# Between the two layers: one block of tokens ahead of the other, values before keys, and the residual's weight and bias on VectorE

## The chip, the cores and the metric

The kernel runs on one core of one Trainium2 chip. A core has a matrix engine (TensorE, "PE" in the profile, with its weight loads as "PEld"), a vector engine (VectorE, "DVE"), an activation engine (ScalarE, "ACT"), GpSimd ("POOL") and SyncE ("SP"), from whose queue every DMA of this kernel is issued. Each engine runs its own instructions in order and waits on semaphores for the others. The metric is the time of one execution on the device in microseconds (us). Three executions of the kernel before took 1293.49, 1297.56 and 1298.24 us; their median is 1297.56.

## The reference: what is computed

256 tokens of width 2048 pass through two layers. The first is a state-space mixer (Mamba-2), the second an attention with three dilated windows. Around each stands the same frame, and between them one matrix of 2048 x 6144 makes the keys and values that the second layer uses:

```python
for layer in range(DEPTH):
    shift, scale, gate = _adaln(c, ada_w[layer], ada_b[layer])
    h = x * (1.0 + scale) + shift
    if layer < N_A_LAYERS:
        y = _ssd_mixer(h, ...)
    else:
        y = _dilated_mixer(h, k_sh, v_sh, b_in_w[i], b_out_w[i])
    x = _layer_norm(DEEPNORM_ALPHA * x + (1.0 + gate) * y, ln_g[layer], ln_b[layer])
    if layer == N_A_LAYERS - 1:
        k_sh, v_sh = _shared_kv(x, kv_w)
```

`_layer_norm` subtracts a token's mean, divides by its standard deviation, multiplies by a weight and adds a bias. `_adaln` is a product of one vector with a matrix of 2048 x 6144 for each layer. Keys and values have three groups of eight heads of 128 each. All numbers are float32.

## The kernel before, in words

**Precision and weights.** A float32 product is made of three products of a shorter format: high part by high part, high by low, low by high. Every weight comes from HBM in pieces of 128 x 1024 words. `split` (lines 90 to 96) makes its high part on ACT (line 93, `whi`) and its low part on DVE (line 95, `wlo`); it has six buffers for raw pieces and four for each part. Activations are kept as high and low parts, too (`xhi`, `xlo`).

**Three forms of product.** `tm_mults` (lines 166 to 176, results with tokens on partitions) takes a block of 128 tokens as PE's stationary operand and streams 512 columns of weights, three matmuls for each block and each 128 of depth; it is used for the state-space layer's z, both output projections and the values. `cm_piece` (lines 109 to 121) and `cm_wide` (lines 140 to 157) have results with channels on partitions: 128 x 128 weights are stationary and tokens are streamed. `cm_piece` streams 256 tokens three times; `cm_wide` streams high and low parts of the tokens together, 512 columns against the weight's high part, then 256 against its low part. Keys must have channels on partitions.

**The step between the layers.** The first layer's output projection (line 683) runs over four chunks of 512 columns with 16 pieces each (two k-tiles of 128 to a piece). In the last chunk the last two pieces are held back (`split_end=2`) and multiplied for block 0 of the tokens first, then for block 1, so block 0's accumulator is complete earlier. `residual` (line 662) multiplies by the gate, adds the scaled input and takes partial moments (lines 664 to 666). `ln_scale` (line 668) makes the factors of both blocks together, with an inverse square root of eleven small DVE steps (lines 209 to 215). Then block 0 is normalised by ACT and block 1 by DVE, in place (lines 701 and 703), and `x_tiles` (line 712) brings the result to channels on partitions: transposes on PE (line 716), weight and bias on ACT into `xhi` (line 719) and on DVE into a copy (line 720), from which the low part is taken (line 721).

**Keys and values.** The keys of the first four heads of each group come first, in the `cm_piece` form, all three groups at once piece by piece (`cm_quads`, line 741), with the next two tiles of x made ahead of each round. Then come the other keys by `cm_wide` and the six value chunks by `tm_chunk` (line 755). Their results go to four large tiles (`kk0`, `kk1`, `vt0`, `vt1`).

**Work in the background.** The modulation (`ada_dot`, line 251) is 48 columns for the second layer, each a DMA of 128 x 2048 words and one DVE instruction. `queue` makes a list of such jobs, and `background` runs some of them after each weight piece: 16 in the output projection, one to three pieces, 32 under the second keys and the values, four to nine pieces. After the values, GpSimd multiplies the residual by the norm's weight and adds its bias (lines 773 and 774), from rows loaded and spread over the partitions.

**Second layer.** `queries` (24 wide pieces for four heads) and `attend` run twice, then `z_gate`, then the output projection. For its end a tile is filled with the gate and the last norm's weight and bias rows (line 850); then two chunks are multiplied, the pieces of the other two are split and held, and block 0 is finished before block 1.

**What sets the order.** A scheduler decides the order on each engine before the run. It takes instructions that are ready by its estimate of time, those that come earlier in the program first, and so may place later work between two dependent steps. `tc.issue_after(ins)` forbids that: what is written in the block on the engine of `ins` is queued behind `ins`. On the chip each engine keeps that order.

## Time and profile before

| | |
|---|---|
| median of three runs | 1297.56 us (1293.49 to 1298.24) |
| the profiled execution's own time | 1296.34 us |
| its span, first to last instruction | 1294.5 us |
| PE busy | 1247.4 us, 96% |
| PE weight loads busy | 1097.5 us, 85% |
| DVE busy | 1027.1 us, 79% |
| ACT busy | 707.7 us, 55% |
| POOL busy | 27.5 us, 2% |
| mean granted PE clock | 0.994 |
| DMA | 335.86 MB, mean 259 GB/s |

The profile is that of one execution. A row of a timeline gives start, duration, engine, line of the kernel and operation, result and operands, shape, and in brackets the idle time before it and what ended that. In the chain a row gives start, the time that it adds, and what. A row of a group ends with busy time, the mean of one in ns and idle time before. A row of windows gives a stretch, its length, then for PE, PEld, DVE, ACT and POOL the busy time with the number of instructions in brackets, and at its end the granted PE clock, the DMA engines' busy share and GB/s. Matmuls are pipelined: their durations overlap, so the distance between two starts is what one of them costs.

The stages by time: the first layer's input and scan up to about 550 us, its output projection to 731, keys and values from 740 to 1015, queries and attention to about 1200, the gate and the second output projection to the end.

### The profile page before, as it was taken

How to read it: one execution, taken by the hardware profiler on the slowest of the kernel's cores; microseconds unless marked ns; L12 is line 12 of the kernel's file. 1: busy time of each engine (PE TensorE's matmuls, PEld its weight loads, DVE VectorE, ACT ScalarE, POOL GpSimd, SP SyncE). 2: the span in 40 equal slices, each digit the busy share in tenths (PEclk: the TensorE clock that was granted, in tenths of full speed). 3: DMA queues.
4: the chain of work that ended last, by engine and by line, in shares of the span. 5: the costliest groups of instructions: out<-in, count | busy, mean ns of one | idle time of the engine just before them, and what ended most of it. 6: DMA issues, size and time to landing. Idle time of an engine off the chain costs nothing.

```text
span 1294.5 us, 19393 instructions
## 1 busy us (share of the span) xinstructions
PE 1247.4 (96%) x7414; PEld 1097.5 (85%) x7414; DVE 1027.1 (79%) x1453; ACT 707.7 (55%) x1033; POOL 27.5 (2%) x20
## 2 busy tenths in 40 slices
PE   4999999999999999999999799999999999999997
PEld 4879988899898999878888699888887888888885
DVE  6789887999999778899765577888777757758778
ACT  3545457867587687864333444444435644444651
POOL 0000000000000000000000043000000000000000
PEclk9999999999999999999999899999999999999999
DMA  9999967696884546398977575999897854363471
GB/s 382 422 398 419 374 210 243 219 342 248 290 313 170 183 161 212 128 338 326 385 258 218 190 238 170 338 393 365 329 342 275 275 187 155 98 187 107 147 276 65
DMA packets 80445, 335.86 MB, mean 259 GB/s; under 512 B 8960, under 2 KB 9056, under 8 KB 67552
## 3 DMA queue, kind: packets, MB, share of 16 engines
q1 hardware_dynamic: 80352, 334.62, 71.5%
q8 instruction: 58, 0.95, 0.3%
q14 instruction: 35, 0.29, 0.1%
HBM read 332.41 MB, written 2.18 MB: 258 GB/s over the span
## 4 chain that ended last, share of the span: by engine, by line
PE 81%; DVE 9%; DMA 5%; ACT 3%; issue 2%; SPq 0%; DVEq 0%; ACTq 0%
PE acc L151 12%; PE acc L174 11%; PE acc L175 11%; PE acc L173 11%; PE acc L121 8%; PE acc L119 8%; PE acc L120 8%; PE acc L152 6%; DMA araw<-in_ada 4%; DVE wlo L95 2%; DVE araw L251 2%; PE py L593 2%; PE aux L802 1%; ACT whi L93 1%; PE po L816 1%
## 5 line engine op out<-in xcount | busy, mean ns | idle before, releaser
L95 DVE TENSOR_TENSOR wlo<-raw,whi 128x1024 fp32r<-128x1024 f32 x395 | 484.4, 1239 | 188.5 <-ACT whi L93 187.5
L93 ACT ACTIVATE whi<-raw 128x1024 fp32r<-128x1024 f32 x395 | 413.0, 1056 | 334.3 <-PE acc L175 139.0
L119 PE MATMUL acc<-actT,whi 128*128 128x256 f32 x960 | 274.1, 289 | 23.2 <-ACT whi L93 19.3
L174 PE MATMUL acc<-wlo,actT 128*128 128x512 f32 x704 | 276.7, 393 | 3.2 <-DVE wlo L95 3.1
L121 PE MATMUL acc<-actT,wlo 128*128 128x256 f32 x960 | 270.8, 286 | 4.4 <-DVE wlo L95 4.4
L173 PE MATMUL acc<-whi,actT 128*128 128x512 f32 x704 | 272.2, 394 | 0.8 <-ACT actT L648 0.7
L120 PE MATMUL acc<-actT,whi 128*128 128x256 f32 x960 | 272.9, 286 | 0.0
L151 PE MATMUL acc<-actT,whi 128*128 128x512 f32 x704 | 251.6, 400 | 0.0
L251 DVE SCALAR_TENSOR_TENSOR araw<-araw,cb__72 128x2048 f32<-128x2048 f32 x96 | 219.3, 2286 | 17.9 <-DMA araw<-in_ada 17.5
L119 PEld LDWEIGHTS acc<-actT,whi 128*128 128x128 f32 x960 | 186.6, 196 | 25.1 <-ACT whi L93 20.3
L152 PE MATMUL acc<-actT,wlo 128*128 128x256 f32 x704 | 201.6, 286 | 0.1
L121 PEld LDWEIGHTS acc<-actT,wlo 128*128 128x128 f32 x960 | 184.6, 194 | 6.7 <-DVE wlo L95 6.4
L120 PEld LDWEIGHTS acc<-actT,whi 128*128 128x128 f32 x960 | 186.7, 194 | 0.4 <-DVE actT L398 0.2
L175 PE MATMUL acc<-whi,actT 128*128 128x512 f32 x448 | 175.0, 391 | 0.0
L174 PEld LDWEIGHTS acc<-wlo,actT 128*128 128x128 f32 x704 | 132.3, 188 | 33.5 <-DVE wlo L95 7.0
L151 PEld LDWEIGHTS acc<-actT,whi 128*128 128x128 f32 x704 | 132.4, 188 | 30.9
L173 PEld LDWEIGHTS acc<-whi,actT 128*128 128x128 f32 x704 | 131.8, 188 | 28.5 <-ACT actT L648 1.5
L152 PEld LDWEIGHTS acc<-actT,wlo 128*128 128x128 f32 x704 | 133.2, 189 | 0.8 <-DVE wlo L95 0.4
L175 PE MATMUL acc<-whi,ylo 128*128 128x512 f32 x256 | 100.3, 392 | 0.0
L175 PEld LDWEIGHTS acc<-whi,actT 128*128 128x128 f32 x448 | 84.1, 188 | 17.1
L175 PEld LDWEIGHTS acc<-whi,ylo 128*128 128x128 f32 x256 | 48.0, 188 | 9.5
L320 DVE SCALAR_TENSOR_TENSOR cacc<-acc,prm,cacc 128x253 f32<-128x253 f32 (+2 forms) x96 | 42.0, 474 | 5.5 <-ACT cacc L317 5.2
(212 smaller groups left out, 1093.0 us busy)
## 6 DMA issues: line engine op xcount, KB each, us to landing
araw<-in_ada SPq DMA_DIRECT2D x96, 1024.0 KB, 7.4
raw<-in_win SPq DMA_DIRECT2D x160, 512.0 KB, 5.3
raw<-in_wkv SPq DMA_DIRECT2D x72, 512.0 KB, 6.2
raw<-in_wout SPq DMA_DIRECT2D x64, 512.0 KB, 4.9
raw<-in_wbin SPq DMA_DIRECT2D x64, 512.0 KB, 4.3
raw<-in_wk SPq DMA_DIRECT2D x24, 512.0 KB, 8.6
cbc<-cumd SPq DMA_DIRECT2D x16, 512.0 KB, 5.4
raw<-in_wbout SPq DMA_DIRECT2D x16, 512.0 KB, 3.7
```

The source lines that it names most:

```text
L93: S.activation(hi, raw, AF.Copy)
L95: latest[0] = V.tensor_tensor(lo, raw, hi.bitcast(F32), op=ALU.subtract)
L119: T.matmul(o, hi[:, k, c_], ahi[:, kt, :], start=first, stop=False, skip_group_check=True)
L120: T.matmul(o, hi[:, k, c_], alo[:, kt, :], start=False, stop=False, skip_group_check=True)
L121: T.matmul(o, lo[:, k, c_], ahi[:, kt, :], start=False, stop=kt == k1 - 1, skip_group_check=True)
L151: T.matmul(ps[n], hi[:, k, c_], xp[:, kt], start=kt == 0, stop=False, skip_group_check=True)
L152: T.matmul(ps[n][:, 0, :], lo[:, k, c_], xhi[:, kt, :], start=False, stop=kt == KT - 1, skip_group_check=True)
L173: T.matmul(o, h_, hi[:, k, :], start=kt == k0, stop=False, skip_group_check=part)
L174: T.matmul(o, h_, lo[:, k, :], start=False, stop=False, skip_group_check=part)
L175: end = T.matmul(o, l_, hi[:, k, :], start=False, stop=kt == k1 - 1, skip_group_check=part)
L251: V.scalar_tensor_tensor(raw, raw, 1.0, cb_, op0=ALU.mult, op1=ALU.mult, accum_out=mod[layer][:, ct, j:j + 1])
L320: V.scalar_tensor_tensor(acc[:, o:], ps[:, :L - o], w[:, j:j + 1], acc[:, o:], op0=ALU.mult, op1=ALU.add)
```

## The change

What it does, in order of the program:

- In the last output chunk four pieces are held for the two blocks instead of two. Each block gets its moments on its own (`moments`, which stood at the kernel's end, with the shorter `rsqrt1`), and its first 512 columns are normalised at once.
- Four pieces of value weights are loaded and split during that chunk (`first_weights`), into the buffers of the first layer's y tiles, which now live in a pool of eight places (`slots`) and later hold keys, values and held weights.
- x is brought to channels on partitions for block 0 alone in its first four tiles; the values of groups 0 and 1 are multiplied for block 0 with the four pieces, then the same for block 1; from the third piece on both blocks go together.
- Values of the first heads come first, then all keys in the wide form, then the other values. `cm_quads` is gone. The wide form does its two 512-column matmuls before its two 256-column ones.
- 11 modulation columns, one to four pieces, lie in the output projection, and 37, one to two pieces, in the keys and values; none in the first two value chunks.
- The residual's norm weight and bias go from GpSimd, after the values, to DVE, one operation after each of 16 pieces of the first queries (`weigh`), with the rows in the buffer that attention uses later (`pT`).
- At the end the gate row is loaded behind the first output chunk, the norm rows behind the second and fourth of the held pieces, and the multiplications by the norm's weight (`scaled`) come behind all the splits.

```diff
@@ cm_wide
                 for n in range(2):
-                    c_ = slice(n * P, n * P + P)
-                    T.matmul(ps[n], hi[:, k, c_], xp[:, kt], start=kt == 0, stop=False, skip_group_check=True)
-                    T.matmul(ps[n][:, 0, :], lo[:, k, c_], xhi[:, kt, :], start=False, stop=kt == KT - 1,
+                    T.matmul(ps[n], hi[:, k, n * P:n * P + P], xp[:, kt], start=kt == 0, stop=False,
+                             skip_group_check=True)
+                for n in range(2):
+                    T.matmul(ps[n][:, 0, :], lo[:, k, n * P:n * P + P], xhi[:, kt, :], start=False, stop=kt == KT - 1,
                              skip_group_check=True)
...
+    slots = ctx.enter_context(tc.tile_pool(name="slots", bufs=1))
...
-        y = [pa.tile([P, 2, 512], F32, name=f"y{g}") for g in range(G)]
+        y = [slots.tile([P, 2, 512], F32, name=f"s{g}") for g in range(G)]
...
+        def moments(b, k, diag=None):
+            mv = sm.tile([P, 2], F32, name=f"e{b}mv", bufs=1)
+            V.bn_aggr(mv, st[b][:, 0:k, :])
...
+            r = rsqrt1(ve, f"e{b}")
...
+        def normalise(b, c0_, c1_):
+            (r, nb), cs_ = norm[b], slice(c0_, c1_)
+            if b == 0:
+                S.activation(u[b][:, cs_], u[b][:, cs_], AF.Identity, bias=nb, scale=r)
+            else:
+                V.tensor_scalar(u[b][:, cs_], u[b][:, cs_], r, nb, op0=ALU.mult, op1=ALU.add)
+
+        def first_weights(q):
+            if q % 3 == 2 and q < 12:
+                i = q // 3
+                into = [slots.tile([P, 1024], F32R, name=f"s{2 * i + j}") for j in range(2)]
+                first_v.append(split(load_piece(wv[2 * (i % 2)][i // 2]), into=into))
...
-                          nk=2 * KT, rate=(1, 3) if n else (0, 1), pre=None if n else y_ahead,
-                          split_end=2 if n == 3 else 0)
+                          nk=2 * KT, rate=(1, 4) if n else (0, 1),
+                          pre={0: y_ahead, 3: first_weights}.get(n), split_end=4 if n == 3 else 0)
             if n == 0:
-                queue(pn, cols1[:16])
+                pin[0] = latest[-3].ins
+                state[0] = 0
+                queue(pn, cols1[:11])
...
                 residual(n, ps[b], b, (gt, u[b][:, 512 * n:512 * n + 512]), xr)
-        drain()
-        r, nb, nb_last = ln_scale()
...
+                if n == 3:
+                    norm.append(moments(b, 4))
+                    normalise(b, 0, 256)
+                    normalise(b, 256, 512)
...
-        cm_quads([(wkv[2 * g], ps[g]) for g in range(NG)], xhi, xlo, pre=ahead, after=nb_last.ins)
...
+        vps = [tm_pair(), tm_pair()]
+        for b in range(2):
+            for kt in range(4):
+                tile4 = x_tile(kt, (b,))
+            for n in range(1, 4):
+                normalise(b, 512 * n, 512 * n + 512)
+            for i, w in enumerate(first_v):
+                if b and i == 2:
+                    x_tile(4)
+                    x_tile(5)
+                tm_mults(i // 2, w, vps[i % 2], hx, lx, 0, KT, (b,))
+        for q in range(2, KT // 2):
+            if q < KT // 2 - 1:
+                x_tile(2 * q + 2)
+                x_tile(2 * q + 3)
+            for j in range(2):
+                w = split(load_piece(wv[2 * j][q]), after=tile4.ins if q == 2 else None)
+                tm_mults(q, w, vps[j], hx, lx, 0, KT, range(2))
+        for g in range(2):
+            evict_v(0, g, vps[g])
+
+        R = (1, 2)
...
+            queue(pl, cols1[11:])
             jobs.append(lambda: gate_out(1))
...
+            evict_v(0, 2, tm_chunk(wv[4], hx, lx, rate=R))
             for hq in range(2):
                 for g in range(NG):
...
+                    for w in range(2):
+                        cm_wide(wk[2 * (2 * g + hq) + w], kv[hq, g][:, 2 * w:2 * w + 2, :], rate=R)
+            for g in range(NG):
+                evict_v(1, g, tm_chunk(wv[1 + 2 * g], hx, lx, rate=R))
...
-                PO.tensor_tensor(u[b][:, cs_], u[b][:, cs_], lnr[0], op=ALU.mult)
-                PO.tensor_tensor(u[b][:, cs_], u[b][:, cs_], lnr[1], op=ALU.add)
...
+    def weigh(n, b, i):
+        if b == 0 and i == 0:
+            t = pc2.tile([P, NG, 384], F32, name="pT", bufs=1).rearrange("p g n -> p (g n)")
+            lnr[n] = [t[:, 512 * j:512 * j + 512] for j in range(2)]
+            for j in range(2):
+                bcast(lnr[n][j], lnrow, j * D + 512 * n)
+        cs_ = slice(512 * n, 512 * n + 512)
+        with tc.issue_after(late):
+            V.tensor_tensor(u[b][:, cs_], u[b][:, cs_], lnr[n][i], op=(ALU.mult, ALU.add)[i])
...
+    jobs.extend(lambda n=n, b=b, i=i: weigh(n, b, i) for n in range(4) for i in range(2) for b in range(2))
...
-                cm_wide(wbin[2 * (2 * g + hq) + w], qq[:, g, 2 * w:2 * w + 2, :])
+                cm_wide(wbin[2 * (2 * g + hq) + w], qq[:, g, 2 * w:2 * w + 2, :], rate=(1, 1))
...
-    bcast(gt[:, 0, :], gated[1])
-    for i in range(2):
-        bcast(lnt[:, i, :], lnrow, (2 + i) * D)
...
         ps = tm_chunk(wbout[n], *og, nk=H)
+        if n == 0:
+            with tc.issue_after(latest[-1].ins):
+                bcast(gt[:, 0, :], gated[1])
         for b in range(2):
             join(n, ps[b], b)
-        scaled(1, chunk[n])
...
+        if i in (1, 3):
+            with tc.issue_after(latest[-1].ins):
+                bcast(lnt[:, i // 2, :], lnrow, (2 + i // 2) * D)
+    for n in range(2):
+        scaled(1, chunk[n])
```

148 lines of the change are left out of this document (52 added, 96 removed).

## The prediction

> **What bounds the kernel now.** I read the page first: its share of busy time, its slices, its chain.
>
> ```profile
> span 1294.5 us, 19393 instructions
> PE 1247.4 (96%) x7414; PEld 1097.5 (85%) x7414; DVE 1027.1 (79%) x1453; ACT 707.7 (55%) x1033; POOL 27.5 (2%) x20
> ...
> PE   4999999999999999999999799999999999999997
> ...
> GB/s 382 422 398 419 374 210 243 219 342 248 290 313 170 183 161 212 128 338 326 385 258 218 190 238 170 338 393 365 329 342 275 275 187 155 98 187 107 147 276 65
> ...
> PE 81%; DVE 9%; DMA 5%; ACT 3%; issue 2%; SPq 0%; DVEq 0%; ACTq 0%
> ```
>
> TensorE (PE) is the bound: it carries 81% of the chain and every slice but the first, the last and the twenty-third is full. That slice, from 712 to 744 us, holds the step between the layers, where the change works. So a microsecond is won only where PE stands still, runs at a lower clock, or spends more per column than it needs. I then read PE's rows in order of time across that step, and the chain there.
>
> ```profile
> 724.33 0.39 PE L175 MATMUL acc<-whi,ylo 128*128 128x512 f32 x1
> ...
> 731.12 0.39 PE L175 MATMUL acc<-whi,ylo 128*128 128x512 f32 x1
> 737.25 1.52 PE L716 MATMUL aux<-cc,u 128*128 128x128 f32 x4 [5.73 <-ACT u L701]
> 740.31 1.65 PE L119 MATMUL acc<-actT,whi 128*128 128x256 f32 x6 [1.54 <-ACT actT L719]
> ```
>
> ```profile
> 731.55 0.70 DVE u L664
> ...
> 736.39 0.17 DVE m01nb L678
> 736.59 3.21 ACT u L701 x5
> ...
> 740.31 1.65 PE acc L119 x6
> 741.96 0.85 PE aux L716 x4
> 742.81 0.21 PE acc L120
> ...
> 752.07 0.44 PE aux L716 x4
> ```
>
> From the first to the last of the 512-column rows are 30 matmuls in 6.79 us, 0.226 each, so the last slot ends at 731.35. The next weight matmul starts at 740.31: **8.96 us** lost to a serial tail of VectorE (DVE), ScalarE (ACT) and four transposes. After it PE is slow: 0.21 a matmul. The granted clock says why:
>
> ```profile
> 735.00:736.00 1.00, 0.00 (x0) 0.00 (x0) 0.81 (x5) 0.00 (x0) 0.00 (x0) 0.76 0.97 401
> ...
> 745.00:746.00 1.00, 1.00 (x7) 1.00 (x7) 1.00 (x2) 0.00 (x0) 0.24 (x1) 0.62 0.85 193
> ```
>
> The third number from the end is the clock. It halves about 4 us after PE stops and is back at about 745.6. From 740.31 to 745.80 PE does 6 + 15 matmuls and four transposes; at the full rates (0.12 below, 0.44 above) that is 21 x 0.12 + 0.44 = 2.96 instead of 5.49. So **2.5 us** more. The step costs 11.5 us in all.
>
> **The change, part by part.**
>
> *One block ahead.* Four held pieces instead of two mean that block 0 ends 4 x 6 x 0.226 = 5.4 us before PE does, at W - 5.4 if W is PE's end. Its residual, moments and first normalisation are the same instructions as those at the kernel's end:
>
> ```profile
> 1270.54 0.24 PE acc L175
> ...
> 1270.80 0.70 DVE actT L664
> ...
> 1275.01 0.17 DVE e0nb L897
> ```
>
> From the last matmul to the ready factor 4.6 us; so W - 0.8, and with a 256-column normalisation (3.21 over five, 0.6 each) block 0's first columns are there at W - 0.2, hidden by block 1's matmuls. The transposes go at W. What then counts is DVE: block 1's chain (again 4.4 us from W + 0.26) stands ahead of block 0's tiles in program order. But the order that is planned slips ready work between dependent steps, as here, where L928 of block 0 goes between L664 and L665 of block 1:
>
> ```profile
> 1276.66 0.68 DVE L664 TENSOR_TENSOR actT<-acc,actT 128x512 f32<-128x512 f32 x1
> 1277.26 0.68 DVE L928 TENSOR_TENSOR u<-u,actT 128x512 f32<-128x512 f32 x1
> 1277.86 0.68 DVE L665 SCALAR_TENSOR_TENSOR u<-u,actT 128x512 f32<-128x512 f32 x1
> ```
>
> ```profile
> L721 DVE TENSOR_TENSOR actT<-xtmp,actT 128x256 fp32r<-128x256 f32 x16 | 9.9, 657 | 0.0
> L719 ACT ACTIVATE actT<-aux,prm 128x256 fp32r<-128x256 f32 x16 | 8.1, 554 | 1.7 <-PE aux L716 1.7
> L720 DVE TENSOR_SCALAR xtmp<-aux,prm 128x256 f32<-128x256 f32 x16 | 7.9, 534 | 0.6 <-ACT actT L719 0.6
> ...
> L703 DVE TENSOR_SCALAR u<-u,m01y,m01nb 128x256 f32<-128x256 f32 x2 | 0.7, 408 | 0.0
> ```
>
> A tile of one block is half of these, about 0.6 us of DVE and 0.3 of ACT (estimates by size). PE can begin about W + 0.9, after two transposes (0.1 each), ACT and two handovers. Of a tile's three products two need only the high part, so PE has 16 of its 24 matmuls while the low parts come between the chain's steps; it is through with block 0 near W + 6.7 (0.9, 5.4 of matmuls, 0.4 of waiting). Block 1's chain, stretched by eight half-tile steps (2.4), gives its factor at W + 7.0, its first columns 0.4 later, its first tile at about W + 8.2: 1.5 of waiting. Behind that, DVE owes three normalisations, tiles 4 and 5 and the first two splits before the fifth piece can end: 0.5. Sum 3.3, none of it long enough to lower the clock. The planned order rests on estimated times and these tails seldom meet so well, so I take 4.5, a gain of 7.0. **Bounds**: nothing lost but the start, 0.9, gain 10.6; or no slipping, where block 0's first low part waits behind block 1's whole chain (0.26 + 4.4 + 0.8 + 0.6 = 6.1, of which PE fills 1.8 with high products), two splits of later pieces cut in (2.5), the clock falls (2.5) and the 0.5 stays: 9.8, gain 1.7.
>
> ```profile
> L95 DVE TENSOR_TENSOR wlo<-raw,whi 128x1024 fp32r<-128x1024 f32 x395 | 484.4, 1239 | 188.5 <-ACT whi L93 187.5
> L93 ACT ACTIVATE whi<-raw 128x1024 fp32r<-128x1024 f32 x395 | 413.0, 1056 | 334.3 <-PE acc L175 139.0
> ...
> L251 DVE SCALAR_TENSOR_TENSOR araw<-araw,cb__72 128x2048 f32<-128x2048 f32 x96 | 219.3, 2286 | 17.9 <-DMA araw<-in_ada 17.5
> ```
>
> ```profile
> 710.00:720.00 10.00, 10.00 (x45) 8.27 (x45) 4.63 (x4) 4.04 (x4) 0.00 (x0) 1.00 0.65 196
> ```
>
> *Four weight pieces split early* into the freed y tiles, in the last output chunk: four loads on SP's queue, 4 x 1.06 us of ACT and 4 x 1.24 of DVE, while five modulation columns of 2.29 leave that layer. DVE is busy 4.63 us of 10 there; zero. Without that cover it is one split, 1.24.
>
> *Values first, keys in the wide form.* Three ways of multiplying, each by rows: 15 matmuls of 256 columns from 812.78 to 814.58, then the stages between the first rows of each kind.
>
> ```profile
> 812.78 0.28 PE L119 MATMUL acc<-actT,whi 128*128 128x256 f32 x1
> ...
> 814.58 0.28 PE L119 MATMUL acc<-actT,whi 128*128 128x256 f32 x1
> ...
> 814.94 0.40 PE L151 MATMUL acc<-actT,whi 128*128 128x512 f32 x1
> 815.18 0.28 PE L152 MATMUL acc<-actT,wlo 128*128 128x256 f32 x1
> 815.29 0.40 PE L151 MATMUL acc<-actT,whi 128*128 128x512 f32 x1
> ```
>
> ```profile
> 814.94:1015.46 200.52, 199.88 (x963) 166.57 (x962) 163.47 (x173) 94.84 (x123) 0.00 (x0) 1.00 0.89 341
> ...
> 1015.46:1083.00 67.54, 67.54 (x384) 58.61 (x383) 37.65 (x44) 31.40 (x42) 0.00 (x0) 1.00 0.64 204
> ```
>
> A piece of 24 narrow matmuls takes 24 x 0.12 = 2.88 us; a wide piece (the second row holds 24) 67.54 / 24 = 2.81; a value piece 12 x 0.226 = 2.72. The 24 narrow pieces of the first keys become wide: 24 x 0.07 = **1.6**. The wide loop's new order (two of 512, two of 256) halves the changes of width. Now a 512 followed by a 256 holds PE 0.24 and a 256 followed by a 512 0.11, where equal neighbours take 0.226 and 0.12; four matmuls go from 0.703 (2.81 / 4) to 0.24 + 0.226 + 0.12 + 0.11, 0.696. That is about 0.025 a piece, **2.8** for the 112 wide pieces of the new kernel. Bounds: 0, or 5.6 if all ran at the rates of equal neighbours; no row prices a loss, since changes only become fewer.
>
> The Trainium skill (TensorE: Matmul & The Clock Gate, Back-to-back issue gap) gives an isolated gap of N/2.4 + 2.5 ns, by which narrow and wide pieces would differ by 8 x 2.5 = 20 ns and the order by nothing: an estimate of 0.5 us instead of 4.4, and 1289 in place of the sum below. The trace does not agree: 0.12 a narrow matmul against 0.109 by that rule.
>
> *More columns behind the keys.* 37 modulation columns instead of 32, one to two pieces instead of four to nine, over 80 pieces. DVE per two wide pieces: two splits 2.48, one column 2.29, one key add 0.41 (the size of L703's): 5.2 of 5.6. DMA: two pieces and a column, 128 x 1024 and 128 x 2048 words of four bytes, 0.52 x 2 + 1.05 = 2.1 MB in 5.4 to 5.6 us, 375 to 386 GB/s; the page's first slices show 422 and 419. Cost zero, bounds: the 2.6 us that this stage loses now (200.52 less 24 x 2.81 and 48 x 2.72) won back, or 7 lost (third rival).
>
> *Weight and bias of the residual* leave GpSimd and its cover under the keys for DVE under the queries: 16 operations of 0.68 (L928 is of the same kind), 11 us where the second window row leaves DVE 30 of 67 free. Zero; the fourth rival prices it.
>
> *The end.* Gate and norm rows are asked for behind the pieces that PE needs first; two multiplications (0.68 each) come later. PE's slices are full until the last one, so nothing; bounds 1 either way, about the two multiplications.
>
> **Sum**: 7.0 + 1.6 + 2.8 = 11.4. The profiled execution took 1296.34 us for its span of 1294.5; less 11.4 is **1285**. The three runs' median, 1297.56, is 1.2 above it.
>
> **Rivals.**
> 1. The step stays, in pieces: block 0's tiles find DVE taken, the clock falls all the same. Gain 1.7 + 1.6 + 2.8, 1290. For: DVE works in order and is taken without a break from W to about W + 14. Against: the slipping shown.
> 2. The forms give nothing: what holds PE beyond its columns is the load of weights, not the number of matmuls or the changes of width, and it comes out alike in each form. Gain 7.0, 1289. For: loads and matmuls overlap, and PEld is busy 85% of the span. Against: in equal neighbours 256 more columns cost 0.226 - 0.12 = 0.106, so a fixed 0.014 a matmul is left over, and a narrow piece pays it 24 times, a wide one 16 times. The rule of the Trainium skill cited above comes to much the same as this rival.
> 3. DMA binds the second part of the keys and values. If 341 GB/s were all it gets, 37 columns with 74 pieces are 77.7 MB, less 5.2 loaded ahead in eight buffers: 213 us against PE's 205.5, 7 lost, 1292. For: the 0.89 share and 341. Against: 422 in other slices.
> 4. Slower: the rows of the residual have one buffer. Each of four pairs can be asked for only after the last operation on the pair before, and lands late:
>
> ```profile
> lnr<-in_lnrow SPq DMA_DIRECT2D x8, 256.0 KB, 5.3
> ```
>
> The next operation is due one piece, 2.8 us, later. If DVE stands on it with the splits of queries queued behind, PE loses up to 4 x 5.3 = 21 us: 1306. It decides from 2.9 us a pair, where the gain of 11.4 is gone. Against: up to four splits ahead, and 30 us of free DVE.
>
> **Numbers.** Forecast 0.60, rivals in order 0.15, 0.10, 0.07, 0.08. Range 1277 to 1294: from the best bounds together (10.6 + 1.6 + 5.6 + 2.6, 1276) to the third rival and the worst bounds of the forecast (1.7 + 1.6, 1293); the fourth is left out. A measurement of this kernel tells about 0.5% from no change, 6.5 us, so faster means below about 1291: 0.58 of the forecast, 0.08 of the second rival and half of the first, 0.73. Same: the rest of these and the third, 0.19. Slower: 0.08.
>
> **What would show it.** Between the last output matmul and the first value matmul about 1 us, with another gap of 1 to 2 before block 1's first tile, and a clock that stays at 1.00. The keys in wide pieces of 2.79 or less. No DVE wait on the row loads under the queries. Wrong if the clock falls in the step, if a DVE wait on modulation columns or rows has a PE gap behind it, or if the wide pieces are no shorter.

## The result

| | before | after |
|---|---|---|
| median of five executions each | 1297.56 us | 1289.79 us (1287.12 to 1292.59) |
| the profiled execution's own time | 1296.34 us | 1289.94 us |
| its span | 1294.5 us | 1287.9 us |
| mean granted PE clock | 0.994 | 0.997 |

The ratio is 0.9942, with a 95% interval of 0.9919 to 0.9965: faster, by 0.6%: 7.8 us on the medians and 6.6 us between the two profiled executions. 11.4 were forecast. The page of the kernel after, in the parts that were shown of before:

```profile
PE 1243.9 (97%) x7222; PEld 1082.4 (84%) x7222; DVE 1031.7 (80%) x1494; ACT 707.7 (55%) x1043; POOL 0.2 (0%) x4
...
PE   4999999999999999999999999999999999999997
```

The slice with the step is full now, and GpSimd's 27 us are gone. The step itself, PE in order of time:

```profile
732.25 0.39 PE L169 MATMUL acc<-whi,ylo 128*128 128x512 f32 x1
732.49 0.38 PE L727 MATMUL aux<-cc,u 128*128 128x128 f32 x2
733.84 0.50 PE L167 MATMUL acc<-s,actT 128*128 128x512 f32 x1 [0.98 <-ACT actT L730]
...
741.39 0.50 PE L167 MATMUL acc<-s,actT 128*128 128x512 f32 x1 [0.44 <-ACT actT L730]
```

PE is through with the output projection at 732.48 and starts on the values 1.36 us later, where it stood still for 8.96 before; ahead of block 1's first tile it waits 0.44. DVE does put block 0's tiles between the dependent steps of block 1's chain:

```profile
735.23 0.34 DVE L731 TENSOR_SCALAR xtmp<-aux,prm 128x128 f32<-128x128 f32 x1
735.49 0.14 DVE L672 TENSOR_SCALAR e1ve<-e1mv 128x1 f32<-128x1 f32 x1
735.55 0.28 DVE L732 TENSOR_TENSOR actT<-xtmp,actT 128x128 fp32r<-128x128 f32 x1
```

The clock stays (third number from the end), and the windows of the two stages behind the first two value chunks show where time was lost again:

```profile
735.00:736.00 1.00, 0.75 (x4) 0.39 (x4) 1.00 (x7) 1.00 (x2) 0.00 (x0) 1.00 0.80 98
...
782.10:1008.21 226.11, 224.25 (x1157) 188.37 (x1156) 190.91 (x207) 105.56 (x143) 0.00 (x0) 1.00 0.92 346
1008.21:1264.03 255.82, 253.83 (x1433) 217.83 (x1432) 182.99 (x318) 122.95 (x187) 0.00 (x0) 1.00 0.55 173
```

In the second row lie 32 value pieces of 2.716 us and 48 wide pieces of 2.787, 220.7 us in all; 5.4 are lost. How, is seen where the key groups stop taking 11.15 us for four pieces and take 11.57. First ACT there, then PE's weight loads and one DVE row:

```profile
871.36 0.66 ACT L150 ACTIVATE s<-acc 128x256 f32<-128x256 f32 x2 [5.16 <-PE acc L146]
871.90 2.95 ACT L93 ACTIVATE whi<-raw 128x1024 fp32r<-128x1024 f32 x3
876.79 1.06 ACT L93 ACTIVATE whi<-raw 128x1024 fp32r<-128x1024 f32 x1 [1.94 <-DMA raw<-in_wk]
882.92 0.66 ACT L150 ACTIVATE s<-acc 128x256 f32<-128x256 f32 x2 [5.07 <-PE acc L146]
```

```profile
877.62 0.30 PEld L146 LDWEIGHTS acc<-actT,wlo 128*128 128x128 f32 x2 [0.59 <-DVE wlo L95]
```

```profile
874.14 2.29 DVE L245 SCALAR_TENSOR_TENSOR araw<-araw,cb__72 128x2048 f32<-128x2048 f32 x1
```

ACT stands 5 us on the eviction of the keys, with the next group's splits queued behind it, then makes three in a row; the fourth waits for its raw piece. DVE puts a dot product of 2.29 us between the low halves, and PE waits for one of them in every group from there on. These groups lose 2.9 us in all, and the three value chunks behind them 1.7 (72.7 us with the last two key pieces, against 71.0 in the run without column loads below). A second loss stands at the start of the second output projection, where the kernel before had none:

```profile
1235.15 0.73 PE L167 MATMUL acc<-whi,s 128*128 128x512 f32 x2 [0.29 <-ACT whi L93]
1237.21 0.50 PE L168 MATMUL acc<-wlo,s 128*128 128x512 f32 x1 [1.33 <-DVE wlo L95]
```

The account between the two profiled executions, stage by stage, from such marks in both. Start to last output matmul: -1.1 us, all of it ahead of the output projection, where the program differs only in where some buffers lie; the output projection takes 181.1 us in both. In that first part the clock falls to half for 3.4 us in the profile before and for 6.8 in the one after. Step: 14.5 us over its matmuls before, 6.2 after, +8.3. Keys: 24 pieces of 2.88 become 2.787 and 24 of 2.827 become 2.787, +3.2. Stalls in the keys and values: 2.3 before, 5.4 after, -3.1. Queries: eleven undisturbed groups at 11.15 and not 11.30, +1.7, and one pause, -0.6. Last query matmul to the end, 56.89 before and 58.84 after: -2.0. Unassigned +0.2. Sum 6.6.

### The profile page after: what moved, and what is told of

It is laid out like the page before. It is cut to its first block, busy times and chain, and to the rows that moved or that the text cites. A ratio compares the mean times of both kernels' runs of the same rounds, so it can differ in the third digit from the quotient of the medians.

```text
span 1287.9 us, 19061 instructions
## 1 busy us (share of the span) xinstructions
PE 1243.9 (97%) x7222; PEld 1082.4 (84%) x7222; DVE 1031.7 (80%) x1494; ACT 707.7 (55%) x1043; POOL 0.2 (0%) x4
## 4 chain that ended last, share of the span: by engine, by line
PE 81%; DVE 9%; ACT 4%; DMA 4%; issue 3%; SPq 0%; DVEq 0%; ACTq 0%
PE acc L143 13%; PE acc L168 12%; PE acc L169 12%; PE acc L167 12%; PE acc L146 7%; PE acc L121 6%; PE acc L120 6%; PE acc L119 6%; DVE araw L245 2%; DVE wlo L95 2%; DMA araw<-in_ada 2%; PE py L590 2%; ACT whi L93 1%; PE aux L832 1%; DMA raw<-in_wk 1%
## 5 line engine op out<-in xcount | busy, mean ns | idle before, releaser
L95 DVE TENSOR_TENSOR wlo<-raw,whi 128x1024 fp32r<-128x1024 f32 x391 | 471.9, 1220 | 154.8 <-ACT whi L93 153.6
L93 ACT ACTIVATE whi<-raw 128x1024 fp32r<-128x1024 f32 x391 | 408.2, 1057 | 331.7 <-PE acc L169 123.0
L143 PE MATMUL acc<-actT,whi 128*128 128x512 f32 x896 | 286.0, 398 | 0.0
L168 PE MATMUL acc<-wlo,actT 128*128 128x512 f32 x688 | 270.4, 393 | 2.8 <-DVE wlo L95 2.5
L167 PE MATMUL acc<-whi,actT 128*128 128x512 f32 x688 | 267.3, 394 | 0.8 <-ACT actT L645 0.7
L119 PE MATMUL acc<-actT,whi 128*128 128x256 f32 x768 | 218.7, 287 | 21.8 <-ACT whi L93 19.3
L121 PE MATMUL acc<-actT,wlo 128*128 128x256 f32 x768 | 217.0, 288 | 4.7 <-DVE wlo L95 4.7
L120 PE MATMUL acc<-actT,whi 128*128 128x256 f32 x768 | 218.7, 286 | 0.6 <-DVE actT L395 0.6
L146 PE MATMUL acc<-actT,wlo 128*128 128x256 f32 x896 | 181.8, 282 | 2.0 <-DVE wlo L95 1.3
L169 PE MATMUL acc<-whi,actT 128*128 128x512 f32 x432 | 168.8, 391 | 0.0
L119 PEld LDWEIGHTS acc<-actT,whi 128*128 128x128 f32 x768 | 149.0, 194 | 23.3 <-ACT whi L93 20.3
L168 PEld LDWEIGHTS acc<-wlo,actT 128*128 128x128 f32 x688 | 129.3, 188 | 32.4 <-DVE wlo L95 7.1
L167 PEld LDWEIGHTS acc<-whi,actT 128*128 128x128 f32 x688 | 128.8, 188 | 27.4 <-ACT actT L645 1.5
L120 PEld LDWEIGHTS acc<-actT,whi 128*128 128x128 f32 x768 | 149.9, 195 | 1.0 <-DVE actT L395 0.8
L143 PEld LDWEIGHTS acc<-actT,whi 128*128 128x128 f32 x896 | 137.6, 189 | 0.3
L169 PEld LDWEIGHTS acc<-whi,actT 128*128 128x128 f32 x432 | 81.1, 188 | 16.5
```

Of the source, the lines that this page charges most:

```text
L93: S.activation(hi, raw, AF.Copy)
L95: latest.append(V.tensor_tensor(lo, raw, hi.bitcast(F32), op=ALU.subtract))
L119: T.matmul(o, hi[:, k, c_], ahi[:, kt, :], start=first, stop=False, skip_group_check=True)
L120: T.matmul(o, hi[:, k, c_], alo[:, kt, :], start=False, stop=False, skip_group_check=True)
L121: T.matmul(o, lo[:, k, c_], ahi[:, kt, :], start=False, stop=kt == k1 - 1, skip_group_check=True)
L143: T.matmul(ps[n], hi[:, k, n * P:n * P + P], xp[:, kt], start=kt == 0, stop=False, skip_group_check=True)
```

## The experiments

Each run is compared with the kernel before on the same chip. A measure that is finer than the median helps: from the first key eviction to the first query eviction lie 12 groups of 11.15 us and 24 value pieces of 2.716, 199.0 us without a stall. The groups of the eviction's line give it for the kernel after, 1020.3 - 816.5, 203.8 us. But for the last two and the run from GpSimd's queue, all medians of changed kernels lie between 1286.5 and 1291.5, and most intervals overlap; where the text tells such kernels apart it goes by rows:

```profile
L150 ACT ACTIVATE qq<-acc x32: 362/371/378, 1020.3 to 1230.5; 128x256 f32<-128x256 f32 x32
L150 ACT ACTIVATE s<-acc x20: 365/379/384, 816.5 to 918.7; 128x256 f32<-128x256 f32 x20
```

| kernel | median us | ratio to before, 95% | key stretch, us |
|---|---|---|---|
| after | 1289.79 | 0.9942 (0.9919 to 0.9965) | 203.8 |
| after, again | 1291.19 | 0.9944 (0.9927 to 0.9961) | 203.9 |
| columns spread | 1287.79 | 0.9923 (0.9901 to 0.9945) | 199.2 |
| no column loads | 1288.49 | 0.9928 (0.9904 to 0.9952) | 199.2 |
| short dot products | 1286.49 | 0.9912 (0.9894 to 0.9930) | 199.7 |
| columns from GpSimd's queue | 1312.42 | 1.0120 (1.0085 to 1.0155) | 220.5 |
| late evictions | 1287.00 | 0.9902 (0.9879 to 0.9925) | 200.5 |
| three column buffers | 1288.13 | 0.9905 (0.9883 to 0.9928) | 203.0 |
| spread and late evictions | 1288.50 | 0.9911 (0.9891 to 0.9931) | 199.2 |
| old order of widths | 1291.52 | 0.9938 (0.9919 to 0.9957) | 204.4 |
| old end | 1288.79 | 0.9919 (0.9897 to 0.9941) | 203.8 |
| two held pieces | 1296.98 | 0.9984 (0.9970 to 0.9997) | 204.0 |
| before, PE kept busy | 1298.43 | 1.0001 (0.9985 to 1.0018) | |

### The loss in the key stage: columns

Fewer columns there, more under the output projection:

```diff
-                          nk=2 * KT, rate=(1, 4) if n else (0, 1),
+                          nk=2 * KT, rate=(4, 11) if n else (0, 1),
...
-                queue(pn, cols1[:11])
+                queue(pn, cols1[:16])
...
-        R = (1, 2)
+        R = (33, 79)
...
-            queue(pl, cols1[11:])
+            queue(pl, cols1[16:])
```

> The changed kernel with its modulation columns as before it: 16 in the output projection (four to eleven pieces), 32 with the gate under keys and values (33 to 79 pieces). The changed kernel loses 5.4 us in the 80 pieces between the first two value chunks and the queries (226.1 us against 220.7 at 2.716 a value piece and 2.787 a key piece); the kernel before lost 2.6 in the like stretch. If the denser columns cost this, by whatever way, the stretch loses 2 to 3.5 and the kernel is 2 to 3 us faster than the changed one, about 1287. If the wide form or the new order of values and keys costs it, it still loses about 5.

Only the first column is loaded in the key stage, and every dot product there reads that one and writes to a second buffer (so the modulation is not the reference's):

```diff
-            raw = loaded.pop(0)
-            if i + 1 < len(cols):
+            raw = loaded[0] if one else loaded.pop(0)
+            if not one and i + 1 < len(cols):
                 loaded.append(ada_load(pool, *cols[i + 1]))
...
-            queue(pl, cols1[11:])
+            queue(pl, cols1[11:], one=True)
```

> Of the 37 modulation columns under keys and values only the first is loaded; every dot product reads that one, so the second layer's modulation is not the reference's. DVE's work is the same. Theory of the queue: on SP's queue a column's load waits at the head until the dot product two before it has freed its buffer, and two pieces' loads stand behind it, so pieces land late; without these loads the 80 pieces lose under 1 us instead of 5.4, and the kernel takes about 1285. Theory of bandwidth: the same, since 39 MB are gone. Theory that DVE is too full (dot products of 2.29 us between the splits): still 4 to 5 lost, 1289.

All columns are loaded, but the dot products there read 128 of their 2048 words:

```diff
-            V.scalar_tensor_tensor(raw, raw, 1.0, cb_, op0=ALU.mult, op1=ALU.mult,
+            w = slice(0, 128 if short[0] else D)
+            V.scalar_tensor_tensor(raw[:, w], raw[:, w], 1.0, cb_[:, w], op0=ALU.mult, op1=ALU.mult,
...
-        R = (1, 2)
+        R, short[0] = (1, 2), True
```

> The 37 columns under keys and values are loaded in full, but the dot product reads only 128 of 2048 words, so the second layer's modulation is not the reference's. Theory that DVE is too full: under 1.5 us lost, 1285 to 1286. Theory of bandwidth: the 5.4 us stay. Theory of the queue: a part is won, since a buffer is freed when the dot product ends, about 2 us earlier, but each load still waits for one: 2 to 4 lost.

The column loads of the stage are issued from GpSimd's queue and no longer from SP's:

```diff
-        nc.sync.dma_start(raw, ada[layer, KIND.index(kind), ct])
+        (PO if own[0] else nc.sync).dma_start(raw, ada[layer, KIND.index(kind), ct])
...
-        R = (1, 2)
+        R, own[0] = (1, 2), True
```

> The columns under keys and values are asked for from GpSimd's queue, where nothing else waits; bytes, buffers and DVE's work are the same. Theory of the queue: the pieces' loads no longer stand behind a column's, ACT's waits for raw pieces (23.0 and 14.9 us now) fall to under half, under 2 us lost, 1286. Theory of bandwidth: the stretch moves the same bytes at the same 346 GB/s and loses 5. Theory that DVE is too full: loses 4 to 5 also.

Measured: the first three each bring the stretch down to 199.2 to 199.7, the floor of 199.0 nearly reached. With short dot products all bytes are still moved, so bandwidth is not the cause; with no loads all the dot products are still there, so DVE's work alone is not it either. The loss needs both. (The schedule of the run without loads even puts more of the dot products into the twelve key groups, as a count further down shows.) ACT's waits in the key stage without the column loads, then with short dot products:

```profile
ACT whi L93 <- PE acc L143: 76.6, 49, 1.8
```

```profile
ACT s L150 <- PE acc L146: 39.0, 8, 7.4
ACT whi L93 <- PE acc L143: 25.1, 16, 1.7
```

Without the loads a split waits only for a buffer that PE frees: the splits are as far ahead as the buffers allow. With short dots ACT stands on its evictions as in the kernel after, but three splits in a row find a DVE that makes their low halves at once, and PE loses nothing.

From GpSimd's queue the stretch is 16.7 us longer than in the kernel after. DVE's waits for columns in that stage, kernel after first:

```profile
DVE araw L245 <- DMA araw<-in_ada: 1.8, 3, 0.8
```

```profile
DVE araw L247 <- DMA araw<-in_ada: 23.5, 19, 3.6
```

No weight piece is late now (ACT has no wait for a raw piece in that stage). DVE works in order, so the low halves stand behind a dot product that waits for its column. But the edit moved more than a queue. DVE's time on dot products while PE multiplies the twelve key groups (a row counts each dot product twice, with the reading of its sum), in the kernel after, without column loads, and from GpSimd's queue:

```profile
804.40:941.00 136.60, 52.74 (x46) 1.00 0.94 354
```

```profile
802.40:935.70 133.30, 66.45 (x60) 1.00 0.62 191
```

```profile
803.20:959.80 156.60, 69.08 (x61) 0.99 0.95 361
```

In both edited runs the scheduler put about 30 dot products there, where the kernel after has 23. Without loads DVE carries them and PE loses nothing. With loads, 31 columns and 48 pieces are 57.7 MB; in the 133.8 us that PE needs for twelve groups this would be 431 GB/s (an estimate), more than the 423 of the page's fullest slice, and 361 were moved. The columns themselves landed 7.5 us after their issue in the median of the stage, 6.9 from SP's queue. So the run loses by its denser order, as far as the rows show; what the queue alone is worth, at the old order, no run shows, and none of the three expectations was met.

### The loss in the key stage: which order keeps it

Key evictions queued behind the third split of the next group:

```diff
+            if q == 2 and put_off:
+                with tc.issue_after(lead[0].ins):
+                    put_off.pop()()
             background(*rate)
-        for n in range(2):
-            S.activation(dst[:, n, :], ps[n][:, 1, :], AF.Copy)
-            V.tensor_tensor(dst[:, n, :], ps[n][:, 0, :], dst[:, n, :], op=ALU.add)
...
+        if put_off is None:
+            evict()
+        else:
+            put_off.append(evict)
```

> The changed kernel, with each pair of key evictions queued on ACT and DVE behind the third split of the group after it and no longer ahead of it. From the first key eviction to the first query eviction the changed kernel took 203.8 us; with fewer columns there, with no column loads, or with short dots it took 199.2, 199.2 and 199.7. Theory A (ACT's order: it stands about 5 us ahead of each eviction with splits queued behind it, so a lead once lost cannot be won again): the stretch falls to 199 to 200 us, and the time by about 4. Theory B (SP's order: a column load stands at the head of SP's queue until the dot product two before it has given its buffer up, and the weight pieces behind it come late): the stretch stays at 203 us or more.

Three column buffers in the key stage:

```diff
-        raw = pool.tile([P, D], F32, name="araw", bufs=2)
+        raw = pool.tile([P, D], F32, name="araw", bufs=deep[0])
...
-        R = (1, 2)
+        R, deep[0] = (1, 2), 3
```

> The changed kernel with three column buffers in the key stage where it has two; same loads, same dot products, same order. Theory B (a column load at the head of SP's queue holds back the weight pieces behind it): SP no longer waits for a dot product there, no split waits for its piece, and the stretch from the first key eviction to the first query eviction falls from 203.8 to 199 to 200 us, the time by about 4. Theory A (ACT's order), and theory C (the dot products themselves keep VectorE from the low halves): the stretch stays at 203 us or more.

The late evictions win 3.3 of the 4.8 us; the third buffer wins 0.8, though SP's waits for column buffers in the stage fall from 114.9 us to 46.3 and no split waits there for a raw piece. With the third buffer the groups take 11.15 us until 893.7, then 12.36 and 11.57. What came there, in ACT's rows with three buffers:

```profile
890.66 0.60 ACT L791 ACTIVATE htmp<-actT,mod 128x256 f32<-128x256 f32 x1 [4.40 <-DVE mod L252]
...
906.04 0.66 ACT L150 ACTIVATE s<-acc 128x256 f32<-128x256 f32 x2 [6.93 <-PE acc L146]
```

The second layer's first modulated tile waits on ACT for DVE's last shift and scale column, with splits behind it. So the trigger differs: late raw pieces in the kernel after, the modulated tile here. What makes it last is the same, as the late evictions show, which have that wait too (1.60) and are back in step one group on:

```profile
886.84 1.09 ACT L801 ACTIVATE htmp<-actT,mod 128x256 f32<-128x256 f32 x2 [1.60 <-DVE mod L260]
...
898.11 1.06 ACT L93 ACTIVATE whi<-raw 128x1024 fp32r<-128x1024 f32 x1 [1.73 <-PE acc L143]
```

Theory A holds for most of the loss, theory B for a small part, and C falls: the dot products are in full in the run with late evictions. In that run no key group loses anything; the 1.3 us that remain lie in the last three value chunks, and no run singles out their cause. The edit moves DVE's additions along with ACT's evictions, so it is the place of the pair that is shown.

Both cures together, beside the changed kernel as it is, on one chip:

> The changed kernel with two things that each gave the key stage back: the modulation columns spread as in the run of that name (16 under the output projection, the rest evenly behind), and the key evictions queued behind the third split of the next group. Theory (one loss, two cures: the lead of the splits): the stretch from the first key eviction to the first query eviction is 199 to 200 us, as with either alone, and the time 1286 to 1287. Rival (two losses that add up, one per cure): the stretch falls below 198 us, and the time to 1284 or less.

> The changed kernel as it is, beside the one that joins the two cures, on the same chip: 1290, with 203.8 us from the first key eviction to the first query eviction if the loss there is the same in every execution; 200 or less if it comes and goes.

The stretch is 199.2, as with the spread alone: one loss, two cures. It is there in both profiled executions of the changed kernel (203.8 and 203.9). By time the two differ by 2.7 us with intervals that overlap, so the times alone don't separate them; the rows do, by 4.7 us. Less is seen in the time because later stages give it back: in the profile of both cures PE waits 1.6 us in the queries, behind DVE's waits for LayerNorm rows, where the second profile of the changed kernel has no such wait, and more at the end, as the next part shows.

### The pause before the second output projection

The kernel before's place and time for the gate and norm rows:

```diff
+    bcast(gt[:, 0, :], gated[1])
+    for i in range(2):
+        bcast(lnt[:, i, :], lnrow, (2 + i) * D)
...
-            with tc.issue_after(latest[-1].ins):
-                bcast(lnt[:, i // 2, :], lnrow, (2 + i // 2) * D)
```

> The changed kernel with the loads of the gate row and of the last two LayerNorm rows, and the tokens scaled by the gate, put back where the kernel before had them (together, ahead of the held pieces). Theory (the rows loaded between the held pieces push the weight pieces of the second output projection back, and the splits queue behind the late one): the pause of 1.3 us for a low half and 0.3 for a high half, near the start of the second output projection, goes, and the time falls by about 1.6 us. Rival (the pause is how four held pieces meet the last query pieces, wherever the rows are loaded): the pause stays at 1 to 2 us and the time stays.

The rows are not the cause of the larger part: the 0.29 goes, the 1.33 stays. The median (1288.79, and 1291.19 for the changed kernel on that chip) doesn't decide, since the intervals overlap.

```profile
1239.62 0.50 PE L168 MATMUL acc<-wlo,s 128*128 128x512 f32 x1 [1.33 <-DVE wlo L95]
```

The widths of the wide form, one line of the diff undone:

```diff
                     T.matmul(ps[n], hi[:, k, n * P:n * P + P], xp[:, kt], start=kt == 0, stop=False,
                              skip_group_check=True)
-                for n in range(2):
                     T.matmul(ps[n][:, 0, :], lo[:, k, n * P:n * P + P], xhi[:, kt, :], start=False, stop=kt == KT - 1,
```

> The changed kernel with one thing undone: in the wide form the two 256-column matmuls follow their own 512-column ones again (512, 256, 512, 256) and no longer come in pairs. Theory (alternating widths cost 0.027 us per wide piece): four wide pieces take 11.25 us again and not 11.15, in all 112 wide pieces, so the kernel is 112 x 0.027 = 3.0 us slower than the changed one, and the queries, which have 64 wide pieces and no column loads, are 1.7 us longer. Rival (the order of the widths costs nothing, and the shorter group came from somewhere else): four pieces stay at 11.15 us and the time stays.

Undisturbed groups of four take 11.30 to 11.31 us again, against 11.15: the order is worth 0.039 us a piece, and the theory is right on that. But the kernel as a whole is not slower than the changed one (0.9938 and 0.9944). The queries are 1.3 us longer, the keys 0.6, and the end 2.1 shorter, since the pause is gone. From 1220 to 1262 us PE is busy for 40.38 of 42 us in the kernel after; with the old order it does not stop:

```profile
1220.00:1262.00 42.00, 42.00 (x206) 35.08 (x205) 32.85 (x37) 22.19 (x26) 0.00 (x0) 1.00 0.68 248
```

ACT's queue, after and then with the old order:

```profile
1230.21 0.64 ACT L150 ACTIVATE qq<-acc 128x256 f32<-128x256 f32 x2
1232.57 1.06 ACT L93 ACTIVATE s<-raw 128x1024 fp32r<-128x1024 f32 x1 [1.73 <-DMA raw<-in_wbout]
...
1234.06 1.99 ACT L93 ACTIVATE whi<-raw 128x1024 fp32r<-128x1024 f32 x2
```

```profile
1235.10 0.38 ACT L149 ACTIVATE qq<-acc 128x256 f32<-128x256 f32 x1 [1.48 <-PE acc L145]
1235.38 1.06 ACT L93 ACTIVATE whi<-raw 128x1024 fp32r<-128x1024 f32 x1
1236.35 0.36 ACT L149 ACTIVATE qq<-acc 128x256 f32<-128x256 f32 x1
```

With the old order the last matmuls of the two accumulators start 0.34 us apart, and the scheduler puts a split for the piece that PE needs next between the two evictions, which so start 1.25 us apart. In the new order the last matmuls stand side by side, the evictions follow each other, and a held piece's split, whose weights are not there yet, comes ahead of that split. That the order of the widths decides is shown: all eleven profiles of the new order have a wait of 1.33 us there, and the three of the old order (the kernel before in two of them) have none. That it does so by this place in the queue is read from the rows, and no run moved that split alone.

The pause has a price of its own. In the profiled execution of the kernel with both cures it is longer, and the clock falls:

```profile
1236.77 0.73 PE L177 MATMUL acc<-whi,s 128*128 128x512 f32 x2 [1.57 <-ACT whi L93]
1238.84 0.80 PE L178 MATMUL acc<-wlo,s 128*128 128x512 f32 x1 [1.33 <-DVE wlo L95]
```

```profile
1238.00:1240.00 2.00, 1.16 (x3) 0.97 (x4) 2.00 (x3) 1.79 (x2) 0.00 (x0) 0.50 0.92 305
```

It is at half from 1238.0 to 1244.8, worth up to 3.4 us. With late evictions alone, and in the second profile of the changed kernel, it is at half for 3.4 us there; in the other profiles of the new order it stays at 1.00.

### The step

Two held pieces where the changed kernel has four:

```diff
-                          pre={0: y_ahead, 3: first_weights}.get(n), split_end=4 if n == 3 else 0)
+                          pre={0: y_ahead, 3: first_weights}.get(n), split_end=2 if n == 3 else 0)
```

> The changed kernel with two held pieces at the end of the output projection where it has four, so that block 0 is through 2.7 us before PE and not 5.4. Theory (block 0's serial tail of 4.6 us and its first normalisation of 0.6 are what the four pieces hide): the first value matmul comes 2.7 us later after the last output matmul, some 4.1 us and not 1.36, and the second pause of 0.44 us goes, since block 1 is ready by then: 2 to 2.7 us slower than the changed kernel, clock at 1.00. Rival (block 1's chain decides, or the order on VectorE): the step as a whole stays within 1 us.

```profile
732.00 0.39 PE L169 MATMUL acc<-whi,ylo 128*128 128x512 f32 x1
736.28 0.44 PE L727 MATMUL aux<-cc,u 128*128 128x128 f32 x2 [3.90 <-ACT u L685]
737.83 0.80 PE L167 MATMUL acc<-s,actT 128*128 128x512 f32 x1 [1.11 <-ACT actT L730]
...
747.35 0.50 PE L167 MATMUL acc<-s,actT 128*128 128x512 f32 x1 [0.44 <-ACT actT L730]
```

```profile
737.00:738.00 1.00, 0.17 (x1) 0.18 (x2) 0.96 (x4) 1.00 (x3) 0.00 (x0) 0.59 1.04 442
...
744.00:745.00 1.00, 1.00 (x6) 0.81 (x5) 0.00 (x0) 0.00 (x0) 0.00 (x0) 0.99 0.00 0
```

It is 5.8 us slower than the changed kernel on the same chip (1296.98 and 1291.19), more than twice what was expected, and not within 1 us as the rival had it. Values start 5.6 us after the last output matmul, not 4.1, since block 1's residual steps now lie between block 0's own dependent steps on DVE:

```profile
732.56 0.22 DVE L220 SCALAR_TENSOR_TENSOR e0t<-e0y,e0ve 128x1 f32<-128x1 f32 x1
732.70 0.69 DVE L661 TENSOR_TENSOR u<-acc,gt 128x512 f32<-128x512 f32 x1
733.30 0.15 DVE L221 SCALAR_TENSOR_TENSOR e0y<-e0t,e0y 128x1 f32<-128x1 f32 x1
```

From residual to factor block 0 takes 5.9 us where it takes 4.4 with four held pieces: the slipping that helps there costs 1.5 here. And the clock, which was to stay, falls and costs the rest: the 512-column matmuls take 0.43 us each until 744. Block 1's chain is stretched alike, and the second pause remains. On that chip the changed kernel gains 7.0 us in all, so most of its gain lies in those two more held pieces.

The kernel before, with 16 matmuls into a spare accumulator behind the output projection:

```diff
         drain()
+        idle = aux.tile([P, 512], F32, name="aux")
+        for i in range(16):
+            T.matmul(idle, yhi[1][:, 15, :P], yp[:, 0, 0:2, :], start=i == 0, stop=i == 15)
         r, nb, nb_last = ln_scale()
```

> The kernel before, with 16 matmuls of 512 columns added right behind the output projection, whose product nothing reads: 3.6 us of work for PE in the 5.7 us in which it waits for the normalisation. Theory (the clock falls about 4 us after PE stops, and the half clock until 745.6 costs 2.5 us): the clock stays at 1.00 through the step, the first 21 key matmuls and four transposes take 3.0 us and not 5.5, and the time falls by about 2.5 us. Rival (the slow matmuls after the step are slow for another reason, such as late low halves): they stay at 0.21 us each and the time stays or rises.

```profile
740.25 1.65 PE L119 MATMUL acc<-actT,whi 128*128 128x256 f32 x6 [1.79 <-ACT actT L722]
```

```profile
733.34:736.76 3.41, 1.74 (x8) 1.12 (x6) 2.93 (x16) 0.22 (x1) 0.00 (x0) 1.00 0.79 257
736.76:740.17 3.41, 0.88 (x4) 0.40 (x4) 3.41 (x7) 3.41 (x7) 0.00 (x0) 1.00 1.01 390
740.17:743.58 3.41, 3.33 (x15) 3.33 (x16) 2.82 (x7) 1.50 (x4) 0.00 (x0) 0.50 0.75 261
```

The clock did not stay. It falls 4.66 us later than in the kernel before and is back 2.2 earlier, so the first matmuls save about 0.9 us of the 2.5; the time shows none of it (1.0001), as 0.9 us lies within its interval. That the slow matmuls are the clock's is borne out by the rows: they go from 0.21 to 0.12 us where the clock is back. In the 3.41 us before it falls, the four transposes are all that PE does, 0.88 us; in the 3.41 us before those PE worked for 1.74, and the clock stayed.

## Why the prediction was right, and where it was off

The forecast was 1285, with 1277 to 1294; 1289.79 lies inside, and faster it is. The sum of 11.4 came out as 7.8 on the medians and as 6.6 between the profiled executions, to which the steps below add up. Of the prediction's own signs of being wrong, two stayed away (the clock in the step, the width of the pieces), and one came in small: a DVE wait on rows with a gap of PE behind it.

**One block ahead** was taken at 7.0, in bounds of 1.7 and 10.6, and gave 8.3. The start came at 1.36 us after the last output matmul where 0.9 was worked out, the second pause was 0.44 where 1.5 was, and the clock stayed. The order slipped tiles between the dependent steps as argued. The point working (3.3 lost, 8.2 gained) was nearer than the value that I took below it for caution. What the working did not say is how near the edge this is: with 2.7 us less of cover the clock falls, and 5.8 us go.

**Forms and order** were taken at 1.6 and 2.8. Keys gave 3.2 and queries 1.7, 4.9 together. The order's 0.025 a piece measured 0.039 in undisturbed groups, but only there: in the groups that are mixed with attention the old and the new order take the same (43.3 and 43.2 us for the first pair), so the price was too low and the number of pieces that gain too high, and that the product came near is luck. The upper bound of 5.6 is too high by the prediction's own rows, (2.81 - 8 x 0.226 - 8 x 0.12) x 112 = 4.7, which moves the range by less than 1 us. The second rival falls. The rule of the Trainium skill cited there (TensorE: Matmul & The Clock Gate, Back-to-back issue gap) makes the order worth nothing, and the trace does not agree: 11.30 against 11.15 us for four pieces.

**More columns behind the keys** was costed at zero, and this is the step that failed: it lost 3.1 us more than before. The count of DVE's time was right, 5.2 of 5.6 us, and so was the bandwidth: with late evictions the stretch from 865 to 930 us runs at 381 GB/s, DVE busy for 58.7 of 65 us, and PE loses nothing. What it left out is what fits between: with so little free, a lead that is lost once is not won back while ACT stands on evictions with splits behind. The third rival had nearly the size of the loss (7, and 5.4 found) and the wrong cause: short dot products end the loss with all the bytes moved.

**The end** was costed at nothing, within 1, and lost 2.0. The loads of the rows, which the prediction had in view, are not the cause of most of it; the new order of widths is, at a place that the prediction did not consider, and it gives back there what it wins in the queries. So two of the named parts, order and end, cancel, as the run with the old order shows.

**Weight and bias on DVE** were costed at zero. The fourth rival came in its mechanism, but small. DVE waits 9.3 us in all for the rows, at most 2.0 at once, and PE stands behind one of these waits for 0.6 us in the queries, where 2.9 lost a pair was the rival's point of decision:

```profile
1043.49 0.69 DVE L809 TENSOR_TENSOR u<-u,pT 128x512 f32<-128x512 f32 x1 [1.30 <-DMA pT<-in_lnrow]
```

```profile
1045.38 0.51 PE L146 MATMUL acc<-actT,wlo 128*128 128x256 f32 x2 [0.32 <-DVE wlo L95]
```

The second profile of the changed kernel has no such pause; the five kernels whose key stage was mended lose 0.8 to 1.9 us there. The first rival falls with the clock at 1.00.

The rest, 1.1 us, is the first layer of the profiled executions, ahead of every line that the change was about.

## What to carry to other kernels

An engine's share of busy time doesn't say whether added work is free: with 5.2 of 5.6 us taken, ask also whether a lead that is lost once can come back, and look for in-order waits (an eviction ahead of the next splits, a load at the head of a queue) that keep it from that. When a change reorders one engine's work, follow the finish times of its results into the queues of the others, to the end of the stage. An edit to a queue can also make the scheduler order another engine anew, so compare that order before reading the time. And a pause of PE has a second price beyond its own length, the half clock behind it; here two more held pieces, 2.7 us of cover, were worth 5.8.

## What the runs showed of the hardware that was not expected

**The clock moves in steps.** From the means of short windows, the clock is at half from 735.5 to 745.8 in the kernel before, 10.2 us; from 737.2 to 744.0 with two held pieces, 6.8; from 740.2 to 743.6 with PE kept busy, 3.4; and at the end 6.8 and 3.4. These are three, two and one times 3.41. The Trainium skill (TensorE: Matmul & The Clock Gate, What's actually happening) states a free-running window of 3413 ns, after which activity or its lack sets the clock; these traces agree on its length. I had read the rows of before as a fall 4 us after PE stops. By steps, what a pause costs depends on where it lies: before the second output projection, pauses of 1.97 and 2.19 us in all (three column buffers, no column loads) cost no step, 2.00 and 2.14 (the changed kernel again, late evictions) one, and 2.90 (both cures) two. How much of a step PE must stand still is seen when all steps at full clock in the 14 profiles are laid out, from 20 us on: in all 5105 in which PE stood still for at most 1.67 us the clock stayed for the next step, in all 31 with more than 1.80 it fell, and of the six between three fell (the ends of matmuls are modelled). So about half of a step is enough, and no idle stretch as long as the step is needed. The same steps make part of the spread between executions: with one of them at half in the first layer its last output matmul starts at 730.3 to 731.2 us, with two at 731.1 to 735.3, with four at 735.5 to 736.3.

**A load in its own queue did not land sooner.** The column loads that held up the weights on SP's queue looked like a fault (114.9 us of SP's waiting in the key stage). Issued from GpSimd's queue they landed 7.5 us after issue in the median, against 6.9, with DMA busy for 0.95 of the key groups' time. The 16.7 us that its key stage lost go, as far as the rows show, with the denser order of dot products that the scheduler made of it.
